# Hybrid decoder layer: the input projection in the order gate, value, q, k, v by channel block, and mixer and output projection in a conv and a head stage

## The chip, the cores and the metric

One Trainium2 chip, of which the program uses one core. The core has a matrix engine (TensorE, PE in the profile, with its weight loads as PEld), a vector engine (VectorE, DVE), an activation engine (ScalarE, ACT), GpSimd (POOL) and a sync engine (SyncE, SP), which issues nearly all transfers. The metric is the device time of one execution in microseconds; less is better.

## The reference

One layer over a sequence of 2048 tokens of 1024 channels, in float32.

```python
a = rmsnorm(x, g_pre_mix);  u = a @ w_in        # 1024 -> 5 x 512 columns
val, gate, q, k, v = split(u)                   # conv value and gate; 8 heads of 64
conv_out = silu(layernorm(causal_depthwise_conv31(val * sigmoid(gate)) + conv_b))
z = q k^T / 8                                   # per head, keys s < t alone
A[t,s] = sigmoid(z[t,s]) * prod_{s<j<t} (1 - sigmoid(z[t,j]))      # stick breaking
attn_out = headwise_rmsnorm(A @ v)
y = concat(conv_out, attn_out) @ w_out          # 1024 -> 1024
h = x + rmsnorm(y, g_post_mix)
f = (silu(fi @ w_gate) * (fi @ w_up)) @ w_down, fi = rmsnorm(h, g_pre_ffn)   # 1024 -> 2816 -> 1024
out = h + rmsnorm(f, g_post_ffn)
```

## The kernel before

Every float32 operand of a large product is split in two parts, H (rounded to the matrix engine's format) and L (the rest), and a product is three matmuls: L with H, H with H, H with L. A matmul has a 128 x 128 stationary operand and 512 moving columns. ACT makes H by a copy, DVE or POOL makes L by a subtraction. Weights come by DMA as `raw` tiles; their L is kept in DRAM after its first use (`wL`).

The tokens are cut in four groups g = 0 to 3 of 512. What runs on PE up to the feed-forward's second half is written by a planner. Its main line is the table `PLAN`, one stage after the other:

- `prep(g)`: the group's normalised input, split into `xH`, `xL`. The pool holds two of each, a half of the channels in each.
- `qkv(g)`, `gv(g)` (function `inproj`): the input projection, one block of 128 output columns at a time (24 matmuls into a PSUM tile `inps`). `qkv` goes q, k, v for head pair 0, then for pair 1 and so on; `gv` goes gate, value for conv channel block 0, 1, 2, 3. q, k and v are stored to DRAM (`qd`, `kd`, `vd`); v is turned first (transposes `vps` into `vt`). For group 0 `gv` comes first, for the others `qkv`.
- `mix(g)`: waits, in the order in which the program is written, until conv and attention of the group are written down; loads the four conv blocks from DRAM (`m<-conv`), takes the four head blocks `ma` from SBUF, and splits all eight into `xH`, `xL`. The tiles `m` belong to a ring of four, `ev`, which `qkH`, `vs`, `vt`, `piece` and others use as well.
- `out(g)` (`outproj`): 192 matmuls `ops` for y, with the conv blocks and the head blocks as separate sums; ACT writes the first sum into the rows `big`, DVE adds the second.
- `fprep(g)`, `c11(g)`, `p4(0)`: input of the feed-forward, and parts of its fast matrix product that need only some of the groups. `c11` is 528 matmuls into tiles `c`.

Three generators run beside the main line (`Side`, `beside`): `attn` (scores `z`, a scan on DVE that makes `om`, a product on POOL that makes `A`, transposes `at`, the split `TH`, `TL`, the sums `o`; at the end of a head `pf` and, of a pair, `po`), `taps` (31 multiply-adds on DVE per conv block, then `convnorm`: transposes `lps`, layer norm, transposes `cps`, and a store by ACT) and `sums` (sums of feed-forward weights, on POOL). `ATTN`, `TAPS` and `SUMS` say how far each shall be when the main line stands at a position; the positions are the third number of `PLAN`'s entries, added up. The items behind it, as `("tprep", 0, 4, 4)`, are small steps put into the stage (what, group, first block, every so many blocks); `tprep` turns columns of group 1's rows and stores their sums, with `piece` tiles. A scheduler then orders the instructions of each engine. When attention and taps are over, the loop over `PLAN` is left; `mix(3)` and `out(3)` follow by themselves, and then the second half (`five`, `slot`), which is the feed-forward's remaining work.

Below, "PE work" is what PE's matmuls and transposes take when they follow each other without a wait.

Of the kernel before, what the change touches and what calls it, by code (L numbers as in the profile page):

```python
# [37 lines left out]

PLAN = (
    ("prep", 0, 6, ("scaled", 0, 0, 0)),  # L40
    ("gv", 0, 44),
    ("qkv", 0, 66, ("stats", 1, 1, 1), ("turned", 1, 8, 1)),
    ("prep", 1, 6),
    ("qkv", 1, 66),
    ("gv", 1, 44, ("stats", 2, 0, 1)),
    ("mix", 0, 0),
    ("out", 0, 44, ("turned", 2, 3, 1)),
    ("prep", 2, 6),
    ("qkv", 2, 66, ("residual", 0, 1, 3)),
    ("gv", 2, 44, ("stats", 3, 0, 1)),  # L50
    ("mix", 1, 0),
    ("out", 1, 44, ("turned", 3, 3, 1)),
    ("prep", 3, 6),
    ("qkv", 3, 66, ("residual", 1, 1, 2)),
    ("gv", 3, 44, ("hscaled", 0, 4, 0)),
    ("fprep", 0, 6),
    ("c11", 0, 121, ("hscaled", 1, 1, 0), ("tprep", 0, 4, 4)),
    ("mix", 2, 0),
    ("out", 2, 44),
    ("p4", 0, 60, ("residual", 2, 2, 2), ("hscaled", 2, 10, 2)),  # L60
    ("fprep", 2, 6),
    ("c11", 2, 121),
)

ATTN = ((100, 0.0), (905, 1.0))
TAPS = ((18, 0.0), (165, 0.168), (200, 0.25), (322, 0.418), (360, 0.5), (480, 0.668), (540, 0.75), (840, 0.918),
        (900, 1.0))
SUMS = ((330, 0.0), (900, 1.0))


# [15 lines left out]
class Side:  # L86
# [11 lines left out]
    def step(self):  # L98

        if self.over or (self.wait is not None and not self.wait()):  # L100
            return False
        self.wait = None
        try:
            r = next(self.gen)
        except StopIteration:
            self.over = True
            return False
# [28 lines left out]
def layer_kernel(ctx: ExitStack, tc: tile.TileContext, x, xT, g_pre_mix, w_in, conv_w, conv_b, ln_g, ln_b,  # L136
# [374 lines left out]
    def mix(g, tiles=None):

        yield need(("conv", g), ("attn", g))
        Hs, Ls = xtiles() if tiles is None else tiles()
        mc[g] = (Hs, Ls)
        for k in range(KT):
            if k < CB:
                m = ev("m")
                nc.sync.dma_start(m, conv[g][:, k, :])
            else:  # L520
                m = ma[g, k - CB]
            H = Hs[k // CB][:, k % CB, :]
            nc.scalar.activation(H, m, AF.Copy)
            nc.vector.tensor_tensor(Ls[k // CB][:, k % CB, :], m, H.bitcast(F32), ALU.subtract)
        done.add(("mix", g))
# [140 lines left out]

    ys = {}

    def outproj(g, rows_, n=2):

        Hs, Ls = mc[g]
        wts = Weights([(w_out, n) for n in range(KT)])
        for e in range(2):
            es = slice(e * G, (e + 1) * G)
            for kp in range(0, CB, n):
                ws = [wts.next() for _ in range(n)]
                for t in range(TT):
                    us = slice(t * P, (t + 1) * P)
                    ps = bank("ops")
                    for i in range(2 * n):  # L680
                        k = 2 * kp + i
                        H, L = (h[k // CB][:, k % CB, us] for h in (Hs, Ls))
                        WH, WL = (m[:, i % 2 * G:(i % 2 + 1) * G] for m in ws[i // 2])
                        nc.tensor.matmul(ps, L, WH, start=i == 0, stop=False)
                        nc.tensor.matmul(ps, H, WH, start=False, stop=False)
                        nc.tensor.matmul(ps, H, WL, start=False, stop=i == 2 * n - 1)
                    if kp == 0:
                        nc.scalar.activation(rows_[t][:, es], ps, AF.Copy)
                    else:
                        nc.vector.tensor_tensor(rows_[t][:, es], ps, rows_[t][:, es], ALU.add)  # L690
                    if t % 2 or n == 1 and t == TT - 1:
                        yield 1 / (1 + (n == 1))
        ys[g] = rows_
        done.add(("out", g))
# [186 lines left out]
    def input_sums(g, k, tmp, banks=bank, t4=None):  # L881

        def turn(k, name):
            ps = banks(name)
            for t in range(TT):
                nc.tensor.transpose(ps[:, t * P:(t + 1) * P], rows["h", (g + 1) * TT + t][:, k * P:(k + 1) * P], id32)
# [37 lines left out]
    def tprep(T):  # L924
        g, k = divmod(T, TT)
        if k == 0:
            t = cm.tile([P, 2, D], F32, tag="big", name="tmp", bufs=2)
            tmp_[:] = [t[:, i // 2, i % 2 * G:(i % 2 + 1) * G] for i in range(4)]
        for _ in input_sums(g, k, tmp_, lambda name: pp.tile([P, G], F32, tag="at", name=name)):
            pass  # L930

    qkv = [(kind, c) for c in range(CB) for kind in ("q", "k", "v")]
    gv = [(kind, c) for c in range(CB) for kind in ("gate", "val")]

    def chain(gens):
        for gen in gens:
# [3 lines left out]
    taps_s = Side(chain(taps(g) for g in range(NG)), 1 / (NG * (CB * CW + 3 * (TAPLAG + LAG * TT))), ("taps", "conv"))  # L940
    sums_s = Side(sums(), 1 / (15 * HF))
    fns = {"prep": (prep, 8), "qkv": (lambda g: inproj(g, qkv), 12), "gv": (lambda g: inproj(g, gv), 8),
           "out": (lambda g: outproj(g, big()), 8), "mix": (mix, 1), "fprep": (ffn_in, 8), "c11": (c11, 2 * HF),
           "p4": (p4, 2 * HF)}
    def each(fn):
        def gen(g):
# [10 lines left out]
    for name, g, cost, *mid in PLAN:  # L957
        fn, total = fns[name]
        pos += cost
        todo = []  # L960
        for what, q, first, every, *some in mid:
            todo += [(first + every * n, t, quick[what], q * TT + t) for n, t in enumerate(some or range(TT))]
        todo.sort(key=lambda e: e[0])

        def due(n):
            while todo and n >= todo[0][0]:
                _, _, f_, q = todo.pop(0)
                f_(q)
# [12 lines left out]
        due(1e9)
    while any([sd.step() for sd, _ in sides]):
# [5 lines left out]
    with ExitStack() as E:  # L988
# [13 lines left out]
        def late():
            ts = operand(*e[0:4])
            return ts[0:2], ts[2:4]

        for _ in mix(NG - 1, late):
# [375 lines left out]
```

## Time and profile before

| what | value |
|---|---|
| median of 3 runs | 2628.95 us (2623.89 to 2630.60) |
| the profiled execution | 2631.28 us, of which the span is 2629.5 us |
| mean granted clock of TensorE | 0.976 |
| busy: PE, DVE, POOL, ACT | 93%, 68%, 56%, 49% of the span |
| moved by DMA | 657 MB, 250 GB/s on average |

A row of a stretch gives its length, then for each engine its busy time and its number of instructions, then the granted clock of TensorE (1.00 is full), the share of time in which the DMA engines are busy, and GB/s. A row of the timeline gives start, duration, engine, line and operation, with the idle time before it and what ended it in brackets.

### The profile page before, as it was taken

How to read it: one execution, taken by the hardware profiler on the slowest of the kernel's cores; microseconds unless marked ns; L12 is line 12 of the kernel's file. 1: busy time of each engine (PE TensorE's matmuls, PEld its weight loads, DVE VectorE, ACT ScalarE, POOL GpSimd, SP SyncE). 2: the span in 40 equal slices, each digit the busy share in tenths (PEclk: the TensorE clock that was granted, in tenths of full speed). 3: DMA queues.
4: the chain of work that ended last, by engine and by line, in shares of the span. 5: the costliest groups of instructions: out<-in, count | busy, mean ns of one | idle time of the engine just before them, and what ended most of it. 6: DMA issues, size and time to landing. Idle time of an engine off the chain costs nothing. (4 is left out here: it accounts for less than half of the span.)

```text
span 2629.5 us, 35727 instructions
## 1 busy us (share of the span) xinstructions
PE 2455.1 (93%) x11156; PEld 1965.3 (75%) x11156; DVE 1791.9 (68%) x2321; ACT 1296.3 (49%) x2398; POOL 1476.4 (56%) x1844
## 2 busy tenths in 40 slices
PE   8989989997999999989999989899999999999998
PEld 6777767785777778767788767677777777887886
DVE  4787479978999576687766535766665665557556
ACT  4455546556565565656656743333323224443543
POOL 6655587557765666547524305765534344557556
PEclk9999999998999999999999989999999999999999
DMA  9999868986798788856776645887665658668664
GB/s 340 327 318 320 269 225 311 359 280 221 253 347 272 244 305 278 294 168 214 262 246 232 224 152 192 311 289 249 215 203 185 200 186 278 194 195 273 207 189 170
DMA packets 289181, 657.31 MB, mean 250 GB/s; under 512 B 33888, under 2 KB 42080, under 8 KB 288992
## 3 DMA queue, kind: packets, MB, share of 16 engines
q1 hardware_dynamic: 264704, 622.01, 70.7%
q10 hardware_dynamic: 24288, 33.04, 3.5%
q8 instruction: 88, 1.44, 0.2%
q14 instruction: 101, 0.83, 0.1%
HBM read 460.92 MB, written 193.99 MB: 249 GB/s over the span
## 5 line engine op out<-in xcount | busy, mean ns | idle before, releaser
L569 POOL TENSOR_TENSOR A<-A,om 128x512 f32<-128x512 f32 (+2 forms) x320 | 314.2, 982 | 352.5 <-DVE om L568 318.5
L568 DVE TENSOR_TENSOR_SCAN om<-om,one,z 128x513 f32<-128x513 f32 (+2 forms) x320 | 351.4, 1112 | 112.8 <-ACT A L566 103.3
L1061 POOL TENSOR_TENSOR wL<-raw,wH 128x512 fp32r<-128x512 f32 x176 | 251.6, 1456 | 304.9 <-issue 156.2
L473 DVE SCALAR_TENSOR_TENSOR cv<-glu,cw,cv 128x512 f32<-128x512 f32 x464 | 346.4, 747 | 5.8
L1241 DVE TENSOR_TENSOR xL__21999<-t__22001,xH__21998 128x512 fp32r<-128x512 f32 x154 | 198.4, 1296 | 160.2 <-ACT xH__21998 L1240 160.1
L1239 POOL TENSOR_TENSOR xL__21997<-t__22000,xH__21996 128x512 fp32r<-128x512 f32 x154 | 208.1, 1357 | 174.5 <-ACT xH__21996 L1238 170.3
L253 PE MATMUL inps<-xH,wL 128*128 128x512 f32 x640 | 261.7, 409 | 3.0 <-DVE qkL L246 2.3
L257 PE MATMUL inps<-xL,wH 128*128 128x512 f32 x640 | 258.5, 405 | 0.0
L255 PE MATMUL inps<-xH,wH 128*128 128x512 f32 x640 | 258.4, 405 | 0.0
L564 ACT ACTIVATE om<-z 128x512 f32<-128x512 f32 (+2 forms) x320 | 171.3, 537 | 162.5 <-DVE z L561 66.4
L246 DVE TENSOR_TENSOR TL<-at,TH 128x512 fp32r<-128x512 f32 (+1 forms) x320 | 189.2, 598 | 89.5 <-ACT TH L245 88.8
L755 PE MATMUL dps<-xH__21996,xL__21999 128*128 128x512 f32 x616 | 241.6, 392 | 7.1 <-DVE xL__21999 L1241 5.7
L755 PE MATMUL dps<-xL__21997,xH__21998 128*128 128x512 f32 x616 | 241.2, 392 | 3.8 <-POOL xL__21997 L1239 3.8
L755 PE MATMUL dps<-xH__21996,xH__21998 128*128 128x512 f32 x616 | 240.9, 391 | 0.0
L839 POOL TENSOR_TENSOR sum<-sum 128x512 f32<-128x512 f32 x132 | 172.6, 1307 | 108.6 <-DMA sum<-in_w_down_dram 39.5
L207 ACT ACTIVATE wH<-raw 128x1024 fp32r<-128x1024 f32 x156 | 165.7, 1062 | 101.2 <-DMA raw<-in_w_in_dram 33.9
L245 ACT ACTIVATE TH<-at 128x512 fp32r<-128x512 f32 (+1 forms) x320 | 167.9, 544 | 91.6 <-PE at L585 83.7
L1238 ACT ACTIVATE xH__21996<-t__22000 128x512 fp32r<-128x512 f32 x154 | 97.1, 631 | 231.8 <-POOL xL__21997 L1239 145.8
L585 PE MATMUL at<-idr,A 128*128 128x128 f32 x1088 | 191.8, 280 | 15.0 <-POOL A L569 4.8
L1060 ACT ACTIVATE wH<-raw 128x512 fp32r<-128x512 f32 x176 | 100.9, 623 | 165.8 <-PE b L755 81.1
L585 PEld LDWEIGHTS at<-idr,A 128*128 128x128 f32 x1088 | 142.2, 144 | 52.7 <-POOL A L569 6.9
L566 ACT ACTIVATE A<-z 128x512 f32<-128x512 f32 (+2 forms) x320 | 167.8, 538 | 21.4 <-PE at L585 17.5
(302 smaller groups left out, 6238.5 us busy)
## 6 DMA issues: line engine op xcount, KB each, us to landing
wL<-wL SPq DMA_DIRECT2D x156, 512.0 KB, 4.8
raw<-in_w_in_dram SPq DMA_DIRECT2D x80, 512.0 KB, 6.2
t__22001<-u SPq DMA_DIRECT2D x154, 256.0 KB, 2.8
c<-c ACTq DMA_DIRECT2D x88, 256.0 KB, 4.1
t__22000<-wd SPq DMA_DIRECT2D x88, 256.0 KB, 2.9
K<-kd SPq DMA_DIRECT2D x80, 256.0 KB, 4.7
V<-vd SPq DMA_DIRECT2D x80, 256.0 KB, 4.0
u<-accf SPq DMA_DIRECT2D x22, 768.0 KB, 4.1
```

The lines of the kernel that those rows point to most:

```text
L246: nc.vector.tensor_tensor(L, ps, H.bitcast(F32), ALU.subtract)
L253: nc.tensor.matmul(ps, WL[:, kc], aH[t](k), start=k == 0, stop=False)
L255: nc.tensor.matmul(ps, WH[:, kc], aH[t](k), start=False, stop=False)
L257: nc.tensor.matmul(ps, WH[:, kc], aL[t](k), start=False, stop=k == KT - 1)
L473: nc.vector.scalar_tensor_tensor(to, gl[c][:, k:k + G], cw[:, c, k:k + 1], a, ALU.mult, ALU.add))
L568: nc.vector.tensor_tensor_scan(r, r, z[:, 0:1].to_broadcast([P, w + 1]), one, ALU.mult, ALU.bypass)
L569: nc.gpsimd.tensor_tensor(a[:, 0:w], a[:, 0:w], om[:, G - w + 1:G + 1], ALU.mult)
L585: nc.tensor.transpose(pt[:, j * P:(j + 1) * P], u["A"][j][:, b * P:(b + 1) * P], id32)
L755: return nc.tensor.matmul(ps, a, b, skip_group_check=True, **flags)
L1061: nc.gpsimd.tensor_tensor(l, t, f32(h), sub)
L1239: nc.gpsimd.tensor_tensor(WL, w, f32(WH), sub)
L1241: nc.vector.tensor_tensor(UL, t, f32(UH), sub)
```

## The change

`gv` and `qkv` of a group become one stage `in` of 20 column blocks, in the order gate, value, q, k, v of block 0, then of block 1, and so on. `mix` and `out` are cut in two: `mixc` and `outc` (the conv blocks and their half of y) and `mixa` and `outa` (the head blocks). `mixed(g, 0)` waits for the group's conv alone and takes one `xH` and one `xL` tile; `mixed(g, 1)` waits for its attention and takes the other two. `mixc(3)` and `outc(3)` become the last entries of `PLAN`, and only `mixa(3)` and `outa(3)` follow behind it. `ATTN` starts and ends earlier, `TAPS` ends at 700 instead of 900, `tprep` is put at blocks 2, 4, 6, 8 of `c11(0)` instead of 4, 8, 12, 16, and `stats` and `turned` get other blocks. A `Side` that runs out now counts its last step as one.

```diff
-    ("qkv", 2, 66, ("residual", 0, 1, 3)),
-    ("gv", 2, 44, ("stats", 3, 0, 1)),
-    ("mix", 1, 0),
-    ("out", 1, 44, ("turned", 3, 3, 1)),
+    ("in", 2, 110, ("residual", 0, 1, 3), ("stats", 3, 15, 1)),
+    ("mixc", 1, 0),
+    ("outc", 1, 22),
+    ("mixa", 1, 0),
+    ("outa", 1, 22, ("turned", 3, 0, 1)),
...
-    ("c11", 0, 121, ("hscaled", 1, 1, 0), ("tprep", 0, 4, 4)),
-    ("mix", 2, 0),
-    ("out", 2, 44),
+    ("c11", 0, 121, ("hscaled", 1, 1, 0), ("tprep", 0, 2, 2)),
+    ("mixc", 2, 0),
+    ("outc", 2, 22),
+    ("mixa", 2, 0),
+    ("outa", 2, 22),
...
     ("c11", 2, 121),
+    ("mixc", 3, 0),
+    ("outc", 3, 22),
 )
-ATTN = ((100, 0.0), (905, 1.0))
+ATTN = ((46, 0.0), (890, 1.0))
+    def mixed(g, part, tiles=xtile):
+        yield need(("attn" if part else "conv", g))
+        H, L = mc[g, part] = tiles()
+        ms = [ma[g, p] if part else ev("m") for p in range(CB)]
...
+    both = [(kind, c) for c in range(CB) for kind in ("gate", "val", "q", "k", "v")]
```

What this does to PE's order is seen at three places. The first is PE where `in(2)` (before: `gv(2)`) ends and the output projection of group 1 waits for conv(1), whose last step on PE are four groups of transposes `cps`. Before, a few rows behind the last matmul `inps` of the stage:

```order
L590 MATMUL o<-TH,V 128x256
L558 MATMUL z<-K,QL 128x512
L559 MATMUL z<-K,QH 128x512
L591 MATMUL o<-TL,V 128x256
L585 MATMUL at<-idr,A 128x128 x4
L590 MATMUL o<-TH,V 128x128
L503 MATMUL cps<-idr,cs 128x128 x4
L591 MATMUL o<-TL,V 128x128
```

Changed, the fourth `cps` stands ahead of the last `inps`:

```order
L258 MATMUL inps<-xH,wH 128x512
L506 MATMUL cps<-idr,cs 128x128 x4
L260 MATMUL inps<-xL,wH 128x512
L594 MATMUL o<-TH,V 128x512
L595 MATMUL o<-TL,V 128x512
```

Before, three of the four `cps` stand behind the last `inps`, and 179 instructions of attention and conv norm (26.5 us of PE work) lie between it and the first `ops`; changed, none of the four does, and the stretch without a large product has 44 instructions (7.1 us).

The second is PE where `c11(0)` ends and the output projection of group 2 starts. Before, the transposes `b_` of the last `tprep` and attention stand ahead of the first `ops`:

```order
L590 MATMUL o<-TH,V 128x512
L591 MATMUL o<-TL,V 128x512
L886 MATMUL b_12250<-idr,hrow 128x128 x4
L590 MATMUL o<-TH,V 128x512
L591 MATMUL o<-TL,V 128x512
L886 MATMUL b_12255<-idr,hrow 128x128 x4
L585 MATMUL at<-idr,A 128x128 x6
L684 MATMUL ops<-wH,xL 128x512
```

```order
L760 MATMUL c_13025<-xL,wH 128x512
L562 MATMUL z<-K,QL 128x512
L563 MATMUL z<-K,QH 128x512
L594 MATMUL o<-TH,V 128x512
L562 MATMUL z<-K,QL 128x512
L563 MATMUL z<-K,QH 128x512
L595 MATMUL o<-TL,V 128x512
L594 MATMUL o<-TH,V 128x512
L589 MATMUL at<-idr,A 128x128 x4
L688 MATMUL ops<-wH,xL 128x512
```

Between the last `c` and the first `ops` stood 84 instructions without a large product (12.6 us of PE work); now it is 11 (2.1 us), and the `tprep` transposes lie inside `c11(0)`.

The third is SP where the loads `m<-conv` of group 1 are issued. Before, the four follow each other; changed, the stores of the last v block (`vt`, of the same ring as `m`) stand between them:

```order
L548 DMA V<-vd_2_197 128x512
L519 DMA m<-conv_3605 128x512 x4
L547 DMA K<-kd_0_145 128x512
L761 DMA wd_5_13622<-sum 128x512
L761 DMA wd_7_13624<-sum 128x512
```

```order
L441 DMA vd_2_199<-vt 128x512
L524 DMA m<-conv_3070 128x512 x2
L772 DMA S_9_(6, 5)_13071<-sum 128x512
L838 DMA sum<-in_w_up_dram 128x512
L524 DMA m<-conv_3070 128x512
L838 DMA sum<-in_w_gate_dram 128x512
L441 DMA vd_2_199<-vt 128x512
L524 DMA m<-conv_3070 128x512
```

The rest of PE's order holds the same matmuls and transposes in both, and from the first product of `five` on it is the same row by row.

More of the change, by code (lines that the diff above doesn't have):

```diff
@@ L40 @@
     ("prep", 0, 6, ("scaled", 0, 0, 0)),
-    ("gv", 0, 44),
-    ("qkv", 0, 66, ("stats", 1, 1, 1), ("turned", 1, 8, 1)),
+    ("in", 0, 110, ("stats", 1, 8, 1), ("turned", 1, 15, 1)),
     ("prep", 1, 6),
[L44 to L47, printed above, removed]
-    ("prep", 2, 6),
-    ("qkv", 2, 66, ("residual", 0, 1, 3)),
-    ("gv", 2, 44, ("stats", 3, 0, 1)),
-    ("mix", 1, 0),
-    ("out", 1, 44, ("turned", 3, 3, 1)),
+    ("in", 1, 110, ("stats", 2, 14, 1)),
+    ("mixc", 0, 0),
+    ("outc", 0, 22),
+    ("mixa", 0, 0),
+    ("outa", 0, 22, ("turned", 2, 0, 1)),
+    ("prep", 2, 6),
+    ("in", 2, 110, ("residual", 0, 1, 3), ("stats", 3, 15, 1)),
[3 more added lines that the diff above has]
+    ("outa", 1, 22, ("turned", 3, 0, 1)),
     ("prep", 3, 6),
-    ("qkv", 3, 66, ("residual", 1, 1, 2)),
-    ("gv", 3, 44, ("hscaled", 0, 4, 0)),
+    ("in", 3, 110, ("residual", 1, 1, 2), ("hscaled", 0, 15, 0)),
     ("fprep", 0, 6),
-    ("c11", 0, 121, ("hscaled", 1, 1, 0), ("tprep", 0, 4, 4)),
-    ("mix", 2, 0),
-    ("out", 2, 44),
+    ("c11", 0, 121, ("hscaled", 1, 1, 0), ("tprep", 0, 2, 2)),
[3 more added lines that the diff above has]
+    ("outa", 2, 22),
     ("p4", 0, 60, ("residual", 2, 2, 2), ("hscaled", 2, 10, 2)),
@@ L62 @@
     ("c11", 2, 121),
-)
-ATTN = ((100, 0.0), (905, 1.0))
-TAPS = ((18, 0.0), (165, 0.168), (200, 0.25), (322, 0.418), (360, 0.5), (480, 0.668), (540, 0.75), (840, 0.918),
-        (900, 1.0))
+    ("mixc", 3, 0),
+    ("outc", 3, 22),
+)
+ATTN = ((46, 0.0), (890, 1.0))
+TAPS = ((30, 0.0), (130, 0.168), (170, 0.25), (260, 0.418), (300, 0.5), (410, 0.668), (450, 0.75), (650, 0.918), (700, 1.0))
 SUMS = ((330, 0.0), (900, 1.0))
@@ L106, in step @@
             self.over = True
-            return False
+            return True
         if callable(r):
@@ L509, in layer_kernel, with xtile @@
     mc = {}
[L511 to L525, printed above, removed]
+    def xtile():
+        return [xp.tile([P, 4, G], F32R, tag=tag, name=tag, bufs=2) for tag in ("xH", "xL")]
+    def mixed(g, part, tiles=xtile):
+        yield need(("attn" if part else "conv", g))
+        H, L = mc[g, part] = tiles()
+        ms = [ma[g, p] if part else ev("m") for p in range(CB)]
+        if not part:
+            for k in range(CB):
+                nc.sync.dma_start(ms[k], conv[g][:, k, :])
+        for k in range(CB):
+            nc.scalar.activation(H[:, k, :], ms[k], AF.Copy)
+            nc.vector.tensor_tensor(L[:, k, :], ms[k], H[:, k, :].bitcast(F32), ALU.subtract)
+        if part:
+            done.add(("mix", g))
         yield 1
@@ L667, in layer_kernel, with outproj @@
     ys = {}
-    def outproj(g, rows_, n=2):
-        Hs, Ls = mc[g]
-        wts = Weights([(w_out, n) for n in range(KT)])
+    def outproj(g, part):
+        H, L = mc[g, part]
+        if not part:
+            ys[g] = big()
+        wts = Weights([(w_out, CB * e + 2 * part + i) for e in range(2) for i in range(2)])
         for e in range(2):
             es = slice(e * G, (e + 1) * G)
[L675 to L694, printed above, removed]
+            ws = [wts.next() for _ in range(2)]
+            for t in range(TT):
+                us = slice(t * P, (t + 1) * P)
+                ps = bank("ops")
+                for k in range(CB):
+                    WH, WL = (m[:, k % 2 * G:(k % 2 + 1) * G] for m in ws[k // 2])
+                    nc.tensor.matmul(ps, L[:, k, us], WH, start=k == 0, stop=False)
+                    nc.tensor.matmul(ps, H[:, k, us], WH, start=False, stop=False)
+                    nc.tensor.matmul(ps, H[:, k, us], WL, start=False, stop=k == CB - 1)
+                y = ys[g][t][:, es]
+                if part:
+                    nc.vector.tensor_tensor(y, ps, y, ALU.add)
+                else:
+                    nc.scalar.activation(y, ps, AF.Copy)
+                if t % 2:
+                    yield 1
+        if part:
+            done.add(("out", g))
     def big():
@@ L928, in tprep @@
             tmp_[:] = [t[:, i // 2, i % 2 * G:(i % 2 + 1) * G] for i in range(4)]
-        for _ in input_sums(g, k, tmp_, lambda name: pp.tile([P, G], F32, tag="at", name=name)):
+        for _ in input_sums(g, k, tmp_):
             pass
@@ L942, in layer_kernel @@
     fns = {"prep": (prep, 8), "qkv": (lambda g: inproj(g, qkv), 12), "gv": (lambda g: inproj(g, gv), 8),
-           "out": (lambda g: outproj(g, big()), 8), "mix": (mix, 1), "fprep": (ffn_in, 8), "c11": (c11, 2 * HF),
+           "in": (lambda g: inproj(g, both), 20),
+           "mixc": (lambda g: mixed(g, 0), 1), "outc": (lambda g: outproj(g, 0), 4),
+           "mixa": (lambda g: mixed(g, 1), 1), "outa": (lambda g: outproj(g, 1), 4), "fprep": (ffn_in, 8), "c11": (c11, 2 * HF),
            "p4": (p4, 2 * HF)}
@@ L978, in layer_kernel @@
                 load_consts(9)
-            if attn_s.over and taps_s.over:
+            if attn_s.over and taps_s.over and (name, g) == PLAN[-1][:2]:
                 break
@@ L1000, in layer_kernel @@
         x2 = [(xp, "xH"), (xp, "xL")]
[L1002 to L1006, printed above, removed]
+        for _ in mixed(NG - 1, 1, lambda: operand(*e[0:2])):
             pass
-        for r in gen:
+        for _ in gen:
             pass
-        for r in outproj(NG - 1, big()):
+        for _ in outproj(NG - 1, 1):
             pass
```

## The prediction

> **What bounds the kernel now.** I read the page's first part, then PE's and DVE's share by stretch, then the timeline where PE stood still, and last the groups.
>
> ```profile
> PE 2455.1 (93%) x11156; PEld 1965.3 (75%) x11156; DVE 1791.9 (68%) x2321; ACT 1296.3 (49%) x2398; POOL 1476.4 (56%) x1844
> ```
>
> PE is the bound, and by this row 174 us of the span are left. But a busy PE is not a PE at its pace, so I measured the pace. The rows give length, PE, PEld, DVE, ACT, POOL, granted clock, DMA share and GB/s.
>
> ```profile
> 1950.00:2000.00 50.00, 50.00 (x214) 39.77 (x213) 32.81 (x39) 12.22 (x21) 18.73 (x13) 1.00 0.59 201
> 1150.00:1200.00 50.00, 50.00 (x250) 41.20 (x249) 37.91 (x56) 29.48 (x53) 19.44 (x39) 1.00 0.46 156
> 422.00:596.00 174.00, 165.20 (x798) 133.08 (x797) 154.03 (x227) 100.80 (x193) 104.19 (x175) 0.98 0.93 321
> 596.00:649.00 53.00, 39.30 (x179) 27.41 (x177) 41.94 (x62) 32.45 (x68) 45.04 (x80) 0.87 0.68 216
> 649.00:724.00 75.00, 68.04 (x310) 54.06 (x311) 70.52 (x101) 43.37 (x80) 51.39 (x73) 0.95 0.75 250
> 725.00:917.00 192.00, 178.17 (x856) 142.87 (x855) 160.70 (x225) 107.48 (x202) 119.24 (x189) 0.96 0.87 291
> 917.00:1102.00 185.00, 182.40 (x901) 148.40 (x900) 121.46 (x160) 111.47 (x202) 108.39 (x149) 1.00 0.84 289
> 1102.00:1132.00 30.00, 20.29 (x86) 12.97 (x84) 24.93 (x38) 15.96 (x31) 15.61 (x28) 0.89 0.68 212
> 1295.00:1313.00 18.00, 14.25 (x79) 9.46 (x77) 17.01 (x24) 14.88 (x27) 5.71 (x12) 1.00 0.97 346
> 1498.00:1531.00 33.00, 19.42 (x77) 12.01 (x75) 16.72 (x21) 14.94 (x27) 9.26 (x16) 0.80 0.18 62
> ```
>
> In 1950 to 2000 only full matmuls run: 50/214 = 0.234 us each. In 1150 to 1200 attention runs beside a large product: 185 full matmuls, ten narrow ones worth 4.5 and 53 transposes, so a transpose is (50 - 189.5 x 0.234)/53 = 0.11 us. By these two prices the whole program is 2340 us of PE work, and some 290 us are lost, not 174. The second row also says that attention loses nothing while a large product stands beside it.
>
> It loses where it is alone. In 596 to 649, 179 instructions (56 full matmuls, 24 narrow ones worth 12, 99 transposes) are 26.5 us of work: 26.5 of 53 us are lost, 1.0 for each us of work. In 1102 to 1132 it is 12.6 us of work in 30 (17.4 lost), in 1498 to 1531, where attention ends, 11.7 in 33 (21.3 lost, 1.8 for each). What such a PE waits for stands in the view of waits:
>
> ```profile
> PE z L558 <- DVE om L568: 30.9, 44, 2.3
> PE o L591 <- DVE TL L246: 23.2, 26, 4.8
> ```
>
> These are attention's own steps on DVE. Two of the three stretches need not be alone. The first waits for conv(1):
>
> ```profile
> 568.31 0.74 DVE L473 SCALAR_TENSOR_TENSOR acc<-glu,cw,cv 128x512 f32<-128x512 f32 x1
> 573.20 0.60 PE L486 MATMUL lps<-idr,acc 128*128 128x128 f32 x4
> 584.28 0.60 PE L503 MATMUL cps<-idr,cs 128*128 128x128 f32 x4
> 638.19 0.60 PE L503 MATMUL cps<-idr,cs 128*128 128x128 f32 x4
> 639.79 0.52 ACTq L506 DMA_DIRECT2D conv<-cs  x1
> 644.53 1.75 SPq L519 DMA_DIRECT2D m<-conv  x4
> 649.25 0.50 PE L684 MATMUL ops<-wH,xL 128*128 128x512 f32 x1 [2.24 <-DVE xL L524]
> ```
>
> The last tap of conv(1) ends at 569, its four conv norm steps take from 573 to 638, 18 us from one `cps` to the next, the last `inps` is over at 596, and the first `ops` comes 11 us after the last `cps`. The second waits for `tprep`:
>
> ```profile
> 1102.59 0.60 PE L886 MATMUL b<-idr,hrow 128*128 128x128 f32 x4
> 1126.22 0.60 PE L886 MATMUL b<-idr,hrow 128*128 128x128 f32 x4
> 1127.64 0.32 SPq L519 DMA_DIRECT2D m<-conv  x1
> 1132.02 0.56 PE L684 MATMUL ops<-wH,xL 128*128 128x512 f32 x1 [0.76 <-DVE xL L524]
> ```
>
> Its `piece` tiles hold the ring from which `m` is taken, so the first `m<-conv` goes out at 1127.6.
>
> **A rule weighed.** In 596 to 649 PE is busy 39.3 of 53 us at a clock of 0.87, for 26.5 us of work. The Trainium skill, Perfetto Trace Analysis, section Identifying the Most-Contended Engine, says that matmul busy time is no good measure of what is left. The trace agrees. Taken by idle time alone (13.7 and 9.7 us in the two stretches) the sum below would come to about -3 us, an estimate. I take the pace.
>
> **The change part by part.** PE's work is the same 2340 us in both orders, and so is the number of instructions on DVE and transfers. From `five` on PE's rows are the same, so nothing is expected behind 1583 us but what the start of it brings.
>
> 1. *Conv(1) earlier, by `in` and `TAPS`.* The stretch without a large product shrinks from 26.5 to 7.1 us of work. The rest of the attention in it goes beside large products, where 1150 to 1200 shows no loss. At 1.0 per us: -19.4 us. Between 0 (conv late again) and -26.5.
> 2. *`tprep` earlier.* 12.6 to 2.1 us of work alone; short ones such as this lose nothing in 1150 to 1200: -17.4. Between -14.5 (lost as before, per us) and -17.4.
> 3. *`outc(3)` inside the plan.* Attention's last stretch is 10.1 us of work instead of 11.7, for `outc(3)` stands between its rows. The end of the chain stays, since `mixa(3)` needs the last head:
>
> ```profile
> 1522.04 0.66 PE L606 MATMUL pf<-idr,oT 128*128 128x128 f32 x4 [0.69 <-ACT oT L655]
> 1527.75 1.09 PE L623 MATMUL po<-idr,ot 128*128 128x128 f32 x4 [5.06 <-DVE ot L615]
> 1530.86 0.80 PE L684 MATMUL ops<-wH,e__17218 128*128 128x512 f32 x1 [2.02 <-DVE e__17218 L524]
> ```
>
>    So 1.6 x 1.8 = -2.9. Between 0 and -6. Half of the output projection now stands ahead of this wait instead of behind it, but it is work either way.
> 4. *A new wait where `in` ends in v.* `mixc` takes its four `m` from the ring that `vs` and the two `vt` still hold, so PE's last `inps` is followed by `vps`, the split, the store of `vt`, and only then the last load. For group 0 the order has 7.4 us of work alone there, where there was none of 2 us before (group 1's 7.1 is in term 1). At 1.0 per us: +7.4. Between 0 and +11, what the same chain took from `cps` to `ops` above.
> 5. *`fprep`.* Its stretches without a large product grow from 11.7 and 11.0 to 14.2 and 12.3 us. The row 1295 to 1313 has 18 us for 11.0, 0.64 lost per us: (2.5 + 1.3) x 0.64 = +2. Between 0 and +4.
> 6. *Taps of group 3 inside `c11(0)`.* DVE's order holds 104 taps there instead of 47, and five more scans and `TL`:
>
> ```profile
> L568 DVE TENSOR_TENSOR_SCAN om<-om,one,z 128x513 f32<-128x513 f32 (+2 forms) x320 | 351.4, 1112 | 112.8 <-ACT A L566 103.3
> L473 DVE SCALAR_TENSOR_TENSOR cv<-glu,cw,cv 128x512 f32<-128x512 f32 x464 | 346.4, 747 | 5.8
> L246 DVE TENSOR_TENSOR TL<-at,TH 128x512 fp32r<-128x512 f32 (+1 forms) x320 | 189.2, 598 | 89.5 <-ACT TH L245 88.8
> ```
>
>    57 x 0.747 + 5 x 1.112 + 5 x 0.598 = 51 us, so DVE has 121.5 + 51 = 172.5 us to do in a stretch of 185. At the highest share that a long row shows, 70.5/75 = 94%, it needs 184 us and costs nothing; at the 154/174 = 89% of 422 to 596, 194 us. I take +7, nearer to the second since that is the longer row. Between 0 and +20 (at the 84% of 725 to 917).
> 7. *Conv norm earlier in PE's queue.* The first `lps` of conv(1) has 452 us of PE work ahead of it instead of 484, while DVE's work ahead of its last tap, counted in DVE's order with the mean of each group, only falls from 441 to 433 us. PE's rows in the trace follow the order of the program, so where `lps` isn't ready, the large products behind it wait too. DVE did the 441 us by 569, a share of 77%; to be in time it needs about 80% of some 545 us. With 89 and 94% seen this is in reach: +4. Between 0 and +24 (32 less 8).
> 8. *Transfers at the start.* q, k and v of the first head pair are stored, and its attention loads, about 3 MB, move ahead into the first 50 us of PE work.
>
> ```profile
> 0.00:50.00 50.00, 40.08 (x165) 31.68 (x166) 24.18 (x33) 25.15 (x36) 31.00 (x46) 1.00 0.95 346
> 450.00:500.00 50.00, 42.55 (x205) 34.30 (x204) 48.30 (x73) 31.30 (x61) 30.36 (x60) 0.93 1.02 384
> ```
>
>    At 346 GB/s and a share of 0.95 there is no room: 3 MB / 346 = 9 us, if the weights queue behind them, nothing if they don't. From 75 us of work on, the sum of bytes is lower than before. I take +2, between 0 and +9. The Trainium skill, DMA: Bandwidth & Descriptors, section Specifications, gives about 358 GB/s as a core's limit of HBM, by which this would be an estimated 8 us; the second row stands above it, at 384, so it is no hard wall here.
>
> The conv loads and the splits of `mixc` and `mixa` are as many as before, and half an output projection (22 us) covers those of `mixa`. `prep`, `turned` and `stats` move by some blocks; PE's order has no more stretches without a large product at them than before, so 0.
>
> Sum: -19.4 - 17.4 - 2.9 + 7.4 + 2 + 7 + 4 + 2 = -17.3 us. The profiled execution took 2631.3 us, 2.3 above the median 2628.95. So 2614 in its terms, 2612 as a median.
>
> **The rivals.**
>
> *The alone work only moves.* All stretches of 2 us and more without a large product add up to 156 us of PE work before and 154 changed, in 41 pieces instead of 34. If each us of it costs what it costs in 596 to 649, the change is worth 2 us: 2627. For it speaks that scheduler and planner spread the same attention; against it, that pieces of 2 to 3 us show no loss in 1150 to 1200.
>
> *DVE becomes the bound (slower).* Terms 6 and 7 both ask DVE for more, sooner. If it can keep no more than the 84% of 725 to 917, `c11(0)` costs +20 instead of +7 and conv(1) is late by 24 us instead of 4: -17.3 + 13 + 20 = +16, so 2645. It decides from a share of about 85% downwards. Against it: 89% over 174 us and 94% over 75.
>
> *The new waits are covered.* If terms 4 to 8 cost nothing, since attention and conv transposes fill them, the sum is -39.7: 2589.
>
> That the change does not do what it says is excluded by the order for terms 1 and 2; only for term 3 may nothing come, 3 us.
>
> **How the numbers follow.** About 0.3% (8 us) is what a measurement of this kernel can tell from no change, so the borders are 2621 and 2637. The forecast, 2601 to 2621, gets 0.50; the covered waits, nearer 2590, 0.16; the alone work that only moves, 2627, 0.18; DVE as the bound, 2645, 0.16. So faster 0.66, same 0.18, slower 0.16. The range goes from 2590, where terms 4 to 8 are nearly nothing, to 2638, about -17.3 with one of the large bounds (term 1 nothing, or term 7 in full) and a few us of term 6; below and above I leave out 2 in 10.
>
> **What would show it.** Where `in(2)` gives way to `outc(1)`, a stretch of some 15 us with little PE instead of 53, and none at the end of `c11(0)`. At the end of `in(1)`, 15 us with half-busy PE, ended by DVE's `xL` behind a late `m<-conv`. DVE at over 90% in `c11(0)`, with PE losing a few us. The wait `po` of 5 us at the end as before. I am wrong if PE waits for `lps` or `cps` inside `in(2)`, or if attention's waits for `om` and `TL` add up to as much as before.

## The result and the profile after

| | median us | runs | ratio to before, 95% interval |
|---|---|---|---|
| before, in the same session | 2626.93 | 2623.89 to 2630.60 | |
| changed | 2603.11 | 2596.21 to 2607.60 | 0.9894 [0.9872, 0.9916] |
| changed, a second time | 2599.68 | 2596.93 to 2604.16 | 0.9891 [0.9873, 0.9910] |

The change makes the kernel 24 us faster (first session), inside the predicted range and 9 us below the predicted 2612. The profiled execution was the shortest of its four, 2596.2 us, so the two traces differ by 35.1 us, 11 more than the medians. The second profile of the changed kernel, 2604.2, was the longest of its four. Below both are used.

The rows that answer to those of before, first the busy time of each engine over the whole span, then the stretches of the changed kernel (length, PE, PEld, DVE, ACT, POOL, granted clock, DMA share, GB/s):

```profile
PE 2434.6 (94%) x11156; PEld 1963.6 (76%) x11156; DVE 1788.6 (69%) x2321; ACT 1292.8 (50%) x2398; POOL 1473.1 (57%) x1844
```

```profile
338.00:358.00 20.00, 12.80 (x57) 9.91 (x56) 14.12 (x23) 10.53 (x24) 14.57 (x26) 0.83 0.96 308
429.00:598.00 169.00, 163.25 (x789) 133.27 (x788) 134.56 (x202) 96.31 (x183) 99.30 (x167) 0.97 0.93 318
598.00:615.00 17.00, 10.98 (x50) 7.57 (x48) 14.83 (x22) 9.95 (x21) 11.31 (x20) 0.90 0.93 313
690.00:865.00 175.00, 166.71 (x804) 135.90 (x803) 143.65 (x206) 96.29 (x182) 104.87 (x168) 0.97 0.87 299
865.00:890.00 25.00, 19.36 (x103) 14.98 (x102) 21.94 (x32) 19.08 (x39) 16.49 (x29) 0.85 1.04 382
890.00:1093.00 203.00, 192.75 (x942) 155.54 (x942) 183.00 (x248) 121.27 (x221) 138.03 (x188) 0.99 0.86 299
1093.00:1095.00 2.00, 2.00 (x11) 1.61 (x10) 2.00 (x4) 1.86 (x4) 0.63 (x4) 1.00 0.84 275
1485.00:1517.00 32.00, 18.62 (x66) 12.96 (x64) 15.31 (x21) 15.01 (x27) 7.91 (x14) 0.69 0.30 106
```

The row 598 to 615 is the old 596 to 649, and the row 1093 to 1095 the old 1102 to 1132: the two long stretches in which attention ran alone are gone. The row 890 to 1093 is the old 917 to 1102, `c11(0)`, and it has become longer. The wait for conv(1) in PE's and SP's timeline of the changed kernel:

```profile
597.83 0.60 PE L506 MATMUL cps<-idr,cs 128*128 128x128 f32 x4
598.18 0.48 PE L260 MATMUL inps<-xL,wH 128*128 128x512 f32 x1
600.87 0.60 PE L435 MATMUL vps<-idr,vs 128*128 128x128 f32 x4
608.13 0.38 SPq L441 DMA_DIRECT2D vd<-vt  x1
608.61 1.30 SPq L524 DMA_DIRECT2D m<-conv  x2
614.91 0.50 PE L688 MATMUL ops<-wH,xL 128*128 128x512 f32 x1 [1.55 <-DVE xL L527]
```

The last `cps` is ahead of the last `inps`, as the order had it. What is left of the wait is the chain that the prediction's term 4 named: v is turned (`vps`), and the store of `vt` at 608.1 stands directly ahead of the first `m` in SP's order. SP's view of waits has 1.1 us for a later `m` that waits until such a store has landed.

Taking PE work (counted along PE's order by the prediction's two prices) from the length of each stage gives what PE lost there. The values come out with 0.10 us for a transpose. With the prediction's 0.11 a stage from input projection 2 on has up to 3 us less, `c11(0)` 15.5 in place of 17.5, and the differences between before and changed move by less than 1 us. The stages, in us lost:

| stage of PE's order | before | changed | changed again |
|---|---|---|---|
| `prep`, input projections 0 and 1, output projection 0 | 60.9 | 54.5 | 58.0 |
| input projection 2, wait for conv(1), output projection 1 | 55.7 | 35.6 | 36.5 |
| input projection 3, `fprep(0)` | 30.5 | 27.0 | 26.6 |
| `c11(0)` | 1.3 | 17.5 | 17.7 |
| its end, output projection 2 | 22.6 | 0.4 | 0.4 |
| `p4`, `fprep(2)`, `c11(2)` | 15.4 | 13.9 | 13.9 |
| end of attention, output projection 3 | 28.8 | 24.4 | 24.5 |
| from `five` on | 53.2 | 59.1 | 62.6 |

Between the two profiles of one kernel the stages from input projection 2 to the end of attention agree within 1 us; the first row and the last differ by 3.5 each. So for this kernel a few us in the middle can be read from one profile, and at the two ends they can't.

### The profile page after: what moved, and what is told of

Its sections match the earlier page's. It is cut to its first block, busy times and chain, and to the rows that moved or that the text cites. A ratio compares the mean times of both kernels' runs of the same rounds, so it can differ in the third digit from the quotient of the medians.

```text
span 2594.5 us, 35632 instructions
## 1 busy us (share of the span) xinstructions
PE 2434.6 (94%) x11156; PEld 1963.6 (76%) x11156; DVE 1788.6 (69%) x2321; ACT 1292.8 (50%) x2398; POOL 1473.1 (57%) x1844
## 5 line engine op out<-in xcount | busy, mean ns | idle before, releaser
L570 ACT ACTIVATE A<-z 128x512 f32<-128x512 f32 (+2 forms) x320 | 168.6, 542 | 19.2 <-PE at L589 14.4
```

## The experiments

Each kernel changes order or tables alone, not what is computed. The first four ask which part of the change does what.

One more line belongs to the change, and the section on it doesn't name it. The transposes of `tprep` no longer go to the PSUM tiles of attention (`at`, two buffers) but to those of `bank`, two buffers that the sums `c` of `c11` use as well:

```diff
-        for _ in input_sums(g, k, tmp_, lambda name: pp.tile([P, G], F32, tag="at", name=name)):
+        for _ in input_sums(g, k, tmp_):
```

Every kernel here with the split has this line; the kernel before, `tprep` alone and `TAPS` alone don't. So no run parts the two. PE's order, which is known without a run, does: with this line alone in the kernel before, 16 instructions (2.6 us of PE work) are left between the last `c` of `c11(0)` and the first `ops`, instead of 84 (12.6 us). With the split alone, without this line and with `tprep` in its old place, it is 117 (17.6 us). The changed kernel with the old tiles would have 156 (23.4 us) there instead of 11.

**`tprep` alone.**

```diff
-    ("c11", 0, 121, ("hscaled", 1, 1, 0), ("tprep", 0, 4, 4)),
+    ("c11", 0, 121, ("hscaled", 1, 1, 0), ("tprep", 0, 2, 2)),
```

> The kernel before with one edit: tprep at blocks 2, 4, 6, 8 of c11(0). Theory A (the 17 us at the end of c11(0) come from tprep's place): the stretch there is gone and the time falls by about 17 us, to some 2610. Theory B (tprep's place only hands the attention on): PE's order no longer has the 12.6 us of small work at the end of c11(0), but its last stretch, where attention ends, holds 33.2 us of small work instead of 11.7. At the 1.0 lost per us seen in the long stretch of in(2) that is 21 us more there, so -17 + 21 = +4: no change that can be told, 2627 to 2635.

2635.60 us, ratio 1.0023 [1.0009, 1.0037]. Stretches of its profile, the border behind `c11(0)` and the end of attention:

```profile
1098.00:1100.00 2.00, 2.00 (x11) 1.63 (x10) 1.97 (x4) 0.97 (x2) 0.29 (x3) 1.00 1.08 383
1462.00:1534.00 72.00, 49.30 (x214) 31.81 (x212) 47.56 (x62) 43.86 (x83) 32.88 (x68) 0.88 0.24 78
```

Theory B, with a time at the upper edge of its range, some 6 us slower than before: the 30 us at the border are 2, and the end has gone from 33 us to 72, of which 38.6 are lost for 33.2 of small work. What isn't done alone at one border is done alone at the next.

**The split alone.**

```diff
-    ("mix", 2, 0),
-    ("out", 2, 44),
+    ("mixc", 2, 0),
+    ("outc", 2, 22),
+    ("mixa", 2, 0),
+    ("outa", 2, 22),
...
```

> The kernel before with the split of mixer and output projection alone (mixc, outc, mixa, outa; outc(3) in the plan; tprep at 2, 4, 6, 8); the stages gv and qkv, ATTN and TAPS stay as before. PE's order: the stretch of small work where conv(1) is awaited stays (24.4 us of work instead of 26.5), the one at the end of c11(0) is gone, the end has 7.1 + 4.5 instead of 11.7. Theory A (the split is what removes the stretch of c11(0), the tables what removes that of conv(1)): about -17 - 2 = -19 us, 2608. Theory B (all of the gain is conv(1) coming earlier): no change, 2627.

The kernel also has `tprep`'s new place and tiles. 2626.17 us, 0.9985 [0.9970, 1.0000]: at most a few us. Its profiled execution, 2614.9, was the shortest of twelve, 11 us under the median. In it, the wait for conv(1), `c11(0)` and the border behind it:

```profile
592.00:645.00 53.00, 37.16 (x169) 25.09 (x167) 39.55 (x58) 30.32 (x63) 41.01 (x72) 0.90 0.70 224
927.00:1113.00 186.00, 182.41 (x890) 147.74 (x890) 125.61 (x166) 112.76 (x206) 113.07 (x153) 1.00 0.83 291
1113.00:1115.00 2.00, 2.00 (x10) 1.61 (x9) 2.00 (x3) 1.54 (x3) 1.20 (x3) 1.00 1.04 395
```

The stretch behind `c11(0)` is gone, and none grows elsewhere (the end of attention is 13 us for 7.1 of small work); the wait for conv(1) stays. The time is theory B's 2627, but not for its reason: part of what is saved behind `c11(0)` is lost again at places where nothing was expected, 8.0 us inside `c11(0)`, and 30.0 instead of 25.2 in input projection 3.

**`in` and the split with the old tables.**

```diff
-ATTN = ((46, 0.0), (890, 1.0))
+ATTN = ((100, 0.0), (905, 1.0))
... (TAPS as before)
```

> The changed kernel with ATTN and TAPS of the kernel before, so the new stage in, the split and tprep's place alone. PE's order: the stretch where conv(1) is awaited is there again (28.4 us of small work); there is none at the end of c11(0); the stretch at the end holds 12.8 + 8.3. Theory A (each stretch costs what it costs in the kernel before): the changed kernel plus some 20 us for conv(1) and some 8 at the end, less the 16 us that c11(0) loses under the early taps: 2603 + 12 = 2615. Theory B (the order gate, value, q, k, v itself is the gain): as the changed kernel, 2603.

2631.15 us, 1.0002 [0.9989, 1.0016]: the whole gain is gone. Its wait for conv(1):

```profile
583.00:647.00 64.00, 46.01 (x191) 31.14 (x189) 44.94 (x67) 35.97 (x76) 47.25 (x82) 0.84 0.69 218
```

36.0 us are lost here for 28.4 of small work, 1.27 for each, so the stretch costs more than theory A gave it; the end of attention and output projection 3 lose 35.6. Theory A's 2615 fails for one reason above all: it took back the 16 us of `c11(0)` with the early taps, but `c11(0)` loses 14.4 here without them. Input projection 3 is at 26, as before the change.

**`TAPS` alone.** The new `TAPS` in the kernel before.

> The kernel before with the new TAPS alone. PE's order: the stretch where conv(1) is awaited shrinks from 26.5 to 7.6 us of small work, but the one at the end of c11(0) grows from 12.6 to 42.1, since mix(2) still waits for conv and attention together and the conv norm of group 3 joins it. Theory A (a stretch costs by its length): -19 + 30 and some us for the taps inside c11(0): +11 to +25, 2640 to 2650. Theory B (earlier taps are the gain by themselves): about -19, 2608.

2669.94 us, 1.0151 [1.0137, 1.0164]. The wait for conv(1), `c11(0)`, and the border behind it:

```profile
601.00:626.00 25.00, 12.01 (x54) 8.74 (x52) 11.72 (x17) 10.71 (x21) 19.78 (x28) 0.72 0.74 241
906.00:1077.00 171.00, 170.06 (x832) 138.95 (x831) 131.79 (x184) 101.11 (x184) 105.18 (x139) 1.00 0.81 272
1077.00:1174.00 97.00, 73.02 (x279) 47.24 (x278) 93.39 (x134) 51.15 (x100) 51.62 (x96) 0.81 0.51 163
```

Conv(1)'s wait falls from 53 to 25 us, but behind `c11(0)` stand 97 us, of which 54.8 are lost, more than theory A's 30, and the time is 20 us above its range. DVE is busy 93.4 of the 97, and PE's largest waits there are for its `om` (12.9 us), so there DVE is the bound. It is the rival "DVE becomes the bound", at another place.

The next four start from the changed kernel.

**`tprep` back.** `("tprep", 0, 4, 4)`.

> The changed kernel with tprep back at blocks 4, 8, 12, 16 of c11(0). tprep by itself brought nothing (2635.6 in the kernel before), so what removes the stretch at the end of c11(0) should be the split. Theory A (the split: mixc(2) waits for conv(2) alone, so attention and tprep can lie beside the products of outc(2)): PE's order has no stretch of small work over 4 us there, and the last one holds 14.1 us instead of 10.1: 0 to +4 us, 2603 to 2607. Theory B (it takes both, tprep's place and the split): the 17 us are back, 2618 to 2620.

2607.54 us, 0.9917 [0.9903, 0.9930], some 6 us over the changed kernel by the ratios, whose intervals overlap. The border behind `c11(0)` of its profile:

```profile
1088.00:1089.00 1.00, 1.00 (x6) 0.82 (x5) 1.00 (x3) 1.00 (x3) 1.00 (x1) 1.00 1.01 283
```

Theory A, as far as it says that `tprep`'s place is not needed: it is worth a few us at most. That the split is what takes the stretch away doesn't follow, for `tprep`'s new tiles are in this kernel too. With the split and the old tiles PE's order would have 270 instructions (41.7 us) here, and this kernel has 3.

**The last block not ending in v.**

```diff
+            for kind in (("gate", "val", "q", "k", "v") if c < CB - 1 else ("q", "k", "v", "gate", "val"))]
```

> The changed kernel with q, k, v, gate, value as the order of the last block alone, so that in(g) ends in the conv value and not in v. PE's order: the 7.4 us of small work where in(1) gives way to outc(0) are gone, the stretch of in(2) stays at 7.3. Theory A (PE waits there for vps, the store of vt and the load of m behind it, as the prediction's term 4): -8 to -12 us, 2591 to 2595. Theory B (the wait of some 11 us there is the end of conv(0), which comes 20 us later when value is last): 2600 to 2615.

2597.93 us, 0.9873 [0.9857, 0.9888]: perhaps 5 us faster than the changed kernel by the ratios, whose intervals overlap, and between the two theories. The end of `in(1)` and output projection 0:

```profile
343.00:345.00 2.00, 0.86 (x4) 0.38 (x2) 0.51 (x1) 1.17 (x3) 0.80 (x4) 1.00 1.03 421
345.00:431.00 86.00, 71.59 (x321) 56.41 (x321) 78.49 (x110) 44.72 (x84) 70.10 (x83) 0.90 0.76 243
```

```profile
PE ops L688 <- DVE xL L527: 6.1, 2, 4.8
```

The 20 us of the changed kernel's row 338 to 358 are 2. But output projection 0 loses 22.6 us instead of 10.5 (the second fence is its view of waits there): it now waits for the conv halves itself. The chain through `vt` is real, but taking it away moves the wait by a few products: up to the end of output projection 0 no less is lost here than in the changed kernel. So a gain of some us would have to lie elsewhere.

**The taps of group 3 late.**

```diff
-... (450, 0.75), (650, 0.918), (700, 1.0))
+... (450, 0.75), (840, 0.918), (900, 1.0))
```

> The changed kernel with the taps of group 3 as late as in the kernel before (0.918 at 840, 1.0 at 900), all else as changed. Theory A (c11(0) loses its 16 us because DVE has the taps of group 3 to do there, 104 instead of 47): c11(0) loses 0 to 3 us again, the end of attention holds 14.4 us instead of 10.1, +4 to +8: together -6 to -12, 2591 to 2597. Theory B (c11(0) loses because attention is denser there, by ATTN): c11(0) as in the changed kernel, 2605 to 2611.

2591.03 us (2584.5 to 2601.1), 0.9856 [0.9835, 0.9878]: the fastest kernel here, some 9 us below the changed one by the ratios, whose intervals just touch. But `c11(0)` of its profile:

```profile
898.00:1098.00 200.00, 191.27 (x930) 155.40 (x929) 142.42 (x190) 117.17 (x217) 135.73 (x182) 0.98 0.88 301
```

DVE is busy 142 of 200 us instead of 183 of 203, and `c11(0)` loses 16.7 instead of 17.5. So DVE's share does not set the loss; the time falls as theory A said, and its mechanism is wrong. PE's waits in `c11(0)` do change, here first the changed kernel and then this one:

```profile
PE z L562 <- DVE om L572: 6.1, 7, 1.4
PE po L627 <- DVE ot L619: 1.6, 1, 1.6
PE b L891 <- DVE hrow L372: 1.0, 1, 1.0
```

```profile
PE b L891 <- DVE hrow L372: 3.9, 2, 2.2
PE c L760 <- ACT c L801: 2.2, 2, 1.8
PE z L562 <- DVE om L572: 1.4, 3, 0.8
```

With the late taps PE waits 4.7 us less for `om` and about as much more for `hrow` (the rows that `tprep` turns) and for `c`: one wait takes the place of another. Its profile, an execution of 2598.9, reaches `five` at 1547.3, the changed kernel's second one at 1546.4: where the gain of the medians lies, the profiles don't show.

**The change without `in`.** `gv` and `qkv` as before, with the split and both new tables.

> The kernel before with the split, tprep's place and both new tables, but with the stages gv and qkv as before: the change without the stage in. PE's order: where conv(1) is awaited 35.0 us of small work, then no stretch at the end of c11(0), 11.7 in fprep(2), and none at the end of attention. Theory A (the table alone moves conv(1) only if gate and value come block by block, as in does): the loss at conv(1) is 35 to 45 us, at the end 0 to 10: 2615 to 2630. Theory B (split and tables are the whole gain): 2603.

2617.77 us, 0.9950 [0.9934, 0.9966]. Its wait for conv(1):

```profile
596.00:672.00 76.00, 56.83 (x238) 38.39 (x236) 60.03 (x87) 45.48 (x93) 60.42 (x105) 0.87 0.64 197
```

Theory A has the time: 41.0 us are lost here, while the end of attention and output projection 3 lose 14.7 instead of 28.8. It does not have the reason: `TAPS` alone left only 7.6 us of small work at this place without `in`, and the split alone 24.4. So it should be the earlier `ATTN` (or its meeting with the split) that makes conv(1) late here, and `in` that lets both tables stand together; `ATTN` alone was not run.

The last four follow from these.

**The changed kernel again.**

> The changed kernel once more, unaltered, beside the three others. Its first profiled execution was the shortest of its runs (2596.2 against a median of 2603.1), and the late taps had 2591.0 as a median beside a profiled execution of 2599. If these are differences from execution to execution, this run gives a median of 2600 to 2607 and a loss in c11(0) of 15 to 19 us as in the first profile.

The table at the top has it: 2599.68, at the lower edge of what was expected, and 17.7 us in `c11(0)`.

**Both faster edits together.**

> The two edits that were faster, together: the last block of in(g) in the order q, k, v, gate, value, and the taps of group 3 as late as in the kernel before. If both gains add (5 and 12 us): 2586. If the late taps only move the wait to the end of attention, which has 21.4 us of small work in PE's order here: 2595 to 2605. The loss in c11(0) stays above 10 us, since its pieces hold 17 us of small work in 50 with or without the taps.

2613.05 us, 0.9941 [0.9924, 0.9958]: slower than either, and above both expectations. `c11(0)` and the end of attention:

```profile
882.00:1093.00 211.00, 196.67 (x939) 157.95 (x938) 143.71 (x191) 119.01 (x219) 132.56 (x183) 0.96 0.84 291
1442.00:1486.00 44.00, 32.77 (x141) 23.02 (x141) 32.39 (x45) 31.32 (x61) 24.77 (x54) 0.84 0.38 118
```

The 21.4 us of small work at the end cost 22.4, as the order let expect, and `c11(0)` loses 26.7.

**Attention thinned in `c11(0)`.**

> The changed kernel with attention held back inside c11(0): ATTN ((46, 0.0), (552, 0.6), (620, 0.640), (890, 1.0)). The taps stay as they are, 104 of group 3 in c11(0). PE's order has 16.3 us of small work in the second 50 us of c11(0) instead of 20.8, and 14.1 us at the end instead of 10.1. Theory A (c11(0) loses because more small work lies beside its products than they cover; the limit is some 14 us in 50): c11(0) loses 8 to 11 us instead of 17; the end of attention costs 0 to 4 more; 2595 to 2603. Theory B (c11(0) loses because the taps fill DVE): c11(0) loses 17 as before, 2603 to 2607.

2600.86 us, 0.9898 [0.9882, 0.9913], the same as the changed kernel. `c11(0)`:

```profile
887.00:1090.00 203.00, 191.51 (x894) 153.66 (x894) 168.93 (x231) 110.76 (x205) 128.00 (x170) 0.95 0.86 302
```

It loses 25.4 us, more than before the edit and not less. The time lies in theory A's range, but the mechanism fails, in the form it had (so much small work per 50 us, so much lost), and theory B's 17 isn't met either. In the first 40 us of `c11(0)` this kernel loses 10.5 us beside 8.5 of small work, and the kernel before 0.4 beside 9.2: the amount of small work is not what sets the loss.

**All tables moved.**

> The last block in the order q, k, v, gate, value, ATTN ((46, 0.0), (392, 0.400), (558, 0.589), (679, 0.709), (870, 1.0)), and the taps of group 3 to 780 and 830. PE's order has no stretch of small work over 4 us where in(2) gives way to outc(1), but 18.2 us of it at the end and 5.8 at the end of in(3). Theory A (each stretch of small work costs 1 us per us): -9 for conv(1), -5 for v, -2 for c11(0), +8 at the end: 2592 to 2598. Theory B (the wait only moves on): 2600 to 2606.

2606.73 us, 0.9923 [0.9903, 0.9943]. The wait for conv(1), then the stages from the end of attention to `five`:

```profile
601.00:606.00 5.00, 2.54 (x15) 1.98 (x14) 2.53 (x5) 2.82 (x6) 1.72 (x5) 0.98 0.93 306
1450.00:1555.00 105.00, 87.58 (x380) 65.61 (x379) 55.53 (x75) 54.33 (x101) 30.45 (x61) 0.90 0.38 131
```

The wait for conv(1) is down to 4.3 us, and output projection 0 loses 23.0, `c11(0)` 25.3, the end 31.0. Theory B, 1 us above its range.

All of them side by side, in us lost. The wait for conv(1) is given with its small work ("26.8 for 26.5"); "behind it" includes output projection 2 and "end of attention" output projection 3:

| kernel | median | at the wait for conv(1) | `c11(0)` | behind it | end of attention |
|---|---|---|---|---|---|
| before | 2628.8 | 26.8 for 26.5 | 1.3 | 22.6 | 28.8 |
| `tprep` alone | 2635.6 | 27.6 for 26.5 | 1.8 | 2.6 | 46.8 |
| `TAPS` alone | 2669.9 | 18.0 for 7.6 | 3.1 | 58.6 | 27.6 |
| split alone | 2626.2 | 28.6 for 24.4 | 8.0 | 0.4 | 27.7 |
| without `in` | 2617.8 | 41.0 for 35.0 | 11.2 | 0.7 | 14.7 |
| old tables | 2631.2 | 36.0 for 28.4 | 14.4 | 1.1 | 35.6 |
| changed | 2603.1 | 9.1 for 7.1 | 17.5 | 0.4 | 24.4 |
| `tprep` back | 2607.5 | 9.3 for 7.1 | 19.2 | 0.8 | 26.2 |
| v not last | 2597.9 | 7.5 for 7.3 | 24.9 | 2.2 | 26.0 |
| late taps | 2591.0 | 9.6 for 7.1 | 16.7 | 0.5 | 27.2 |
| both edits | 2613.1 | 8.2 for 7.3 | 26.7 | 0.4 | 40.9 |
| thinned | 2600.9 | 7.7 for 7.1 | 25.4 | 0.9 | 26.6 |
| all tables | 2606.7 | 2.5 for 1.8 | 25.3 | 0.4 | 31.0 |

## Why the prediction was right, and where it was not

The sign and the main mechanism hold. None of the parts that were run is the whole: the new order without the tables brings 0, the split alone about 4 us, the taps alone cost 41, all but `in` brings some 13. `ATTN` alone, `in` alone and `tprep`'s new tiles alone were not run. Both tables together bring conv(1) forward only with `in`. What keeps early taps from piling up behind `c11(0)` is by PE's order `tprep`'s new tiles: with them `TAPS` alone has 1 instruction there instead of 277, but then 44.9 us of small work stand at the end of attention.

The prediction's 2340 us of PE work and 290 lost are miscounted: its two prices as printed give 2362 and 268 for the 11156 instructions. No term of the sum uses them.

- **Term 1, conv(1) earlier: -19.4 predicted, -17.7 measured** (26.8 to 9.1; -18.4 in the second profile). The price of 1.0 per us of small work alone was right for the long stretch. Over the five kernels of the table with over 20 us of it there, it runs from 1.0 to 1.3.
- **Term 2: -17.4 predicted, -17.4 at its place** (17.1 to -0.3). The cause was wrong, so it was luck that the size fits: I gave it to `tprep`'s place. `tprep` alone brings the same stretch back at the end of attention, and with `tprep` back in its old place the stretch stays away. Nor is it the split by itself: in PE's order `tprep`'s new tiles take the stretch away without the split, and the split does not without the tiles. How much time the tiles are worth by themselves stays open.
- **Term 6: +7 predicted, +16.2 measured, the largest mistake.** I took DVE's share as the measure, with the taps as the load. With late taps DVE's share falls from 90% to 71% and the loss stays. I had also said that attention "loses nothing while a large product stands beside it", from one row of 50 us, of which 15 are small work; and the price of a transpose was worked out from that same row, so it could show no loss. The three kernels with the old `mix` lose 1.3 to 3.1 us in `c11(0)`, the ten with the split, 8.0 to 26.7. So of the 22 us saved behind `c11(0)`, the changed kernel gives 16 back inside it. They lie in its first 120 us, some 10 of them with PE standing still, for `om`, `po` and `hrow` above all, as in the view of waits further up.

  What sets the loss stays open. More small work lies beside the products in the ten (30 to 39 us in the first 100 us of PE work, against 23 to 28), but thinning it did not lower the loss. The ten are also the kernels with `tprep`'s new tiles, and with the old tiles PE's order would have 24 to 28 us there. In the traces `c` waits for a step of `tprep` that holds such a tile (`tmp`), but for little: 0.4 us in the changed kernel, 0.9 in the split alone, 2.2 without `in`. A run of the changed kernel with the old tiles would tell the split and the tiles apart, and there is none.
- **Term 3: -2.9 predicted.** The stretch itself has hardly become shorter:

```profile
1508.56 0.66 PE L610 MATMUL pf<-idr,oT 128*128 128x128 f32 x4 [0.69 <-ACT oT L659]
1514.27 1.09 PE L627 MATMUL po<-idr,ot 128*128 128x128 f32 x4 [5.05 <-DVE ot L619]
1517.38 0.79 PE L688 MATMUL ops<-wH,e__17289 128*128 128x512 f32 x1 [2.02 <-DVE e__17289 L527]
```

  From `pf` to `ops` it is 8.82 us in both kernels, and 32.2 us hold 10.1 of small work where 32.6 held 11.7. A price per us of work was the wrong form: here a chain of fixed length decides. The whole end still fell by 4.4, all of it in what runs behind the stretch, which now is half an output projection.
- **Term 4: +7.4 predicted, 11.5 and 10.6 at its place**, the upper bound. But output projection 0 lost 10.5 instead of 16.8, and `in(0)` and `in(1)` less than `gv` and `qkv`: the first row of the stage table is 6.4 and 2.9 lower. That the wait shows up in `outc(0)` when v isn't last fits this: it moves by a few products, and only some us of it are v's.
- **Terms 5, 7, 8.** `fprep(0)` lost 11.1 instead of 5.3, so 5.8 and not 2 (and `fprep(2)` 0.9 less). No wait for `lps` inside `in(2)`: that stage lost 14.1 instead of 16.8, so term 7 was 0 or less. The first 100 us of work lost 15.4 and 16.2 instead of 19.2; the transfers moved there cost nothing. The new wait there is another one, `inps` for the gate's sigmoid:

```profile
PE z L562 <- DVE om L572: 30.5, 38, 3.8
PE inps L256 <- ACT sg L422: 10.3, 4, 4.3
PE o L595 <- DVE TL L249: 8.4, 10, 1.7
PE po L627 <- DVE ot L619: 6.9, 3, 5.0
```

  The waits for `om` are as long in sum as before (30.5 and 30.9 us); those for `TL` fell from 23.2 to 8.4, so the two together are shorter, 38.9 instead of 54.1, and the sign of being wrong did not show.
- **Not costed:** input projection 3 lost 15.9 instead of 25.2. It loses less in each of the seven kernels with `in` and both tables' early part (15.0 to 23.7), and in none without (25.2 to 31.5). So it takes `in` and the tables: with `in` and the old tables it is 26, with the tables and without `in` as well. Why is not shown.
- **From `five` on** the order is the same row by row, and the prediction put 0. The profiles have 1046 us before, 1052 and 1056 changed, and 1042 in the kernel with all tables moved:

```profile
1583.00:2629.00 1046.00, 995.06 (x4258) 800.83 (x4256) 637.87 (x677) 394.70 (x714) 574.86 (x436) 0.99 0.67 222
```

```profile
1542.00:2594.00 1052.00, 999.58 (x4257) 804.27 (x4255) 636.49 (x677) 397.07 (x718) 571.29 (x436) 0.98 0.67 221
```

  One execution can't tell whether that is the change or the execution.

So the sum of -17.3 stands against -24 in the medians and -36 and -28 in the lost times of the two profiles, and that it came so near is in part luck, for errors cancelled. One term was right (1) and one right in size for another reason (2). Too little loss was put down for `c11(0)` (9 us), `fprep` (3), term 4 (4) and the work from `five` on (6 and 9). Gains that the sum did not have stood against them: 9 us in input projection 3, 6 in output projection 0, 5 in output projection 2, and some 12 from the terms 7 and 8, which cost nothing.

The Trainium skill, Perfetto Trace Analysis, section Optimization Strategy, says that a kernel in which the busiest engine changes over time may gain by interleaving its regimes. The trace agrees at conv(1), where DVE (41.9 us) was busier than PE (39.3 us) and 53 us became 17. In `c11(0)` the trace shows a limit: 16 of the 22 us saved behind it are lost inside it.

## What to carry to other kernels

Look in the order for stretches where small, chained work runs alone on PE; where they are long, each us of work in them costs another 1.0 to 1.3. Removing one is worth that only if its work finds room: ask where it goes. In `tprep` alone it stood at the next barrier, and in the changed kernel part of its cost came back inside the product ahead. Read every line of a change before giving an effect to one of them: here one line, on which tiles a small step writes to, decides by PE's order what stands behind `c11(0)`. And where two edits each gain, run them together before adding them up: by their ratios to before, 5 and 9 us faster alone were 13 slower together.

## What was not expected of the hardware

The half clock behind a long wait makes the wait dearer than its idle time. After the 5.05 us before `po` in the fence above, the granted clock from 1515 to 1521 is 0.50, and the first products of `outa(3)` follow each other at 0.43 us instead of 0.234. In timeline and stretch:

```profile
1519.25 0.63 PE L689 MATMUL ops<-wH,e__17288 128*128 128x512 f32 x1
1519.68 0.63 PE L690 MATMUL ops<-wL,e__17288 128*128 128x512 f32 x1
```

```profile
1515.00:1521.00 6.00, 3.98 (x11) 2.85 (x10) 4.37 (x8) 4.84 (x9) 0.00 (x0) 0.50 0.13 21
```

The Trainium skill, TensorE: Matmul & The Clock Gate, section Part 1: The HAM clock gate, has this as half rate after one idle window of about 3.4 us. The trace agrees: the products of `outa(3)` go at half pace from 1517.4 to 1521.0, 3.6 us, and the same pace of 0.43 us stands behind the 3.80 us that PE waited for `om` before 1491.2. Over the 32 us of this stretch the granted clock is 0.69, which is part of why 10.1 us of small work take so long. A single long gap is not needed, though. In `TAPS` alone no wait of PE between 1077 and 1174 is longer than 1.3 us, and still one row of it has half the clock while PE is busy 5.45 of 6 us:

```profile
1107.00:1113.00 6.00, 5.45 (x16) 3.75 (x16) 6.00 (x14) 2.58 (x7) 2.58 (x10) 0.50 0.22 52
```
